# The order of the weight quarters and the modulation blocks in the first product of a two-layer encoder

## The chip, the cores and the metric

The kernel runs on one core of one Trainium2 chip. The metric is the time of one execution on the device in microseconds; the time of a kernel is the median of its runs. The profile is that of one further execution.

## The reference

The kernel computes a two-layer bidirectional encoder on 256 tokens of width 2048, all in float32. What matters here is the beginning of each layer:

```python
cond = jax.nn.silu(c)
mod = cond @ w_ada[l] + b_ada[l]                   # 2048 -> 6 * 2048
sh_a, sc_a, g_a, sh_m, sc_m, g_m = split(mod, 6)
h = _rmsnorm(x) * (1.0 + sc_a) + sh_a
proj = h @ w_in[l]                                 # 2048 -> 3904 columns
```

`proj` is cut into queries, keys and values of a differential attention and into the small latents of a second attention; both attentions, an output projection and a squared-ReLU MLP follow, and then the second layer. The change touches layer 0's part of the lines shown.

## The kernel before

**Tiles.** Everything is held transposed: features on the 128 partitions, the 256 tokens along the free axis. The 2048 features are 16 blocks of 128 ("k"), and the first product takes them two at a time, as pairs 0 to 7 (`p`, with `k = 2 * p`).

**Modulation.** `w_ada` is read as blocks of 128 outputs by 2048 inputs, 1 MB each. `ada_load` issues one such load on SyncE's queue (L294); `ada_sums` has VectorE multiply the block with `cond` and sum along the free axis (L304, two instructions: the product and the read of its sum). After the second block of a pair a small instruction adds the bias (L317 for a shift, L315 for a scale). A pair of feature blocks needs two blocks of the shift ("sh", group 0) and two of the scale ("sc", group 1). `ada_todo` lists them in the order sh, sh, sc, sc, pair by pair. `ada_need(l, g, i)` loads and sums everything in that list up to block `i` of group `g`.

**The operand.** `modulated` makes the two blocks of a pair: `ht` is x times scale times the reciprocal norm (VectorE, L646); the high part of `h` comes from ScalarE (L649) and the low part from VectorE (L650), so that a product can be done as three fast ones (high by high, high by low, low by high). For pairs 0 to 5 (`WHOLE = 6`) ScalarE also makes an unsplit copy `hf` (L654).

**The products of a pair.** `by_k` multiplies the pair's rows of the weights with the operand and adds into open PSUM banks. For pairs 0 to 5 the weights are used unsplit (L233 loads them into four tiles, L244 multiplies). For pairs 6 and 7 `weights` loads a raw tile (L163), ScalarE makes its high part (L148) and VectorE its low part (L151), in two halves, and `mac` issues the three matmuls (L187, L188, L189). Here `io["w_a"]` holds two column groups of 768, `b = 0` and `b = 1`.

**The second columns.** Another 512 columns of the first product, `io["w_d"]`, come as four quarters, each for four feature blocks, always split. Below they are called q0 to q3. `EARLY` says that q0 is done behind pair 4, q1 behind pair 5, q2 behind pair 6; q3 comes behind pair 7. So q0 to q2 use only feature blocks that have long been made.

**Buffers.** Raw tiles and modulation blocks share five buffers of 1 MB (`tag="raw"`); a buffer comes free when VectorE has summed the block or subtracted both halves of the weights. High and low parts have four buffers each (`tag="hi"`, `tag="lo"`), which the unsplit weights of pairs 0 to 5 use as well; they come free when TensorE is through with them.

**What sets the order.** Each engine, and SyncE's queue of loads, works in order. A planner writes that order out before the run: it goes through the program with estimated durations and gives each engine, of the instructions that it takes to be ready, the one that stands first in the program. `follow(ins, after)` forces an order between two instructions of one engine. In the kernel before, at the end of pairs 4, 5 and 6, the program has first all four modulation blocks of the next pair (`ada_need` for sh and sc), then the quarter (`early[p]`), then the next pair's operand. The variable `self.lo` is the last low part that was made, `self.summed` the last sum of a modulation block.

`norm_then_by_k` is called once more, for the MLP of layer 0, with `early` empty.

## Time and profile before

| | |
|---|---|
| median of 3 runs | 2191.54 us (2191.27 to 2192.47) |
| the profiled execution | 2190.2 us |
| its span | 2188.4 us |
| granted TensorE clock, mean | 0.995 |
| TensorE busy (matmuls) | 2158.3 us, 99% |
| VectorE busy | 1610.4 us, 74% |
| ScalarE busy | 1153.3 us, 53% |
| sums of modulation blocks, L304 | 192, of 2284 ns |
| moved by DMA | 586.41 MB, 268 GB/s in the mean |

A row of a timeline reads: start in us from the span's start, duration, engine, line of the kernel, operation, output<-inputs with their shapes, how many in a row; in brackets, how long the engine stood idle before it, and what ended that. PE is TensorE, DVE VectorE, ACT ScalarE, SPq SyncE's queue of loads. A row of a table by stretches reads: the stretch, its length, busy time (and instructions) of PE, of its weight loads, of DVE, ACT and POOL, the granted TensorE clock, the share of DMA, GB/s. The layer's first product lies between 24 us and 152 us of the span.

### The profile page before, as it was taken

Reading aid. Unit: us, or ns where it says so; the run is one execution under the profiler, and the core shown is the slowest. Engines: PE = TensorE matmul, PEld = TensorE weight load, DVE = VectorE, ACT = ScalarE, POOL = GpSimd, SP = SyncE. Lnnn points to the kernel's source line nnn. Section 1 sums busy time; section 2 is a strip of 40 time slices with the busy share of each in tenths; the row PEclk is TensorE's granted clock in tenths of the full one; section 3 lists DMA queues with packets and bytes.
Section 4 is the critical chain, followed back from the end, with each engine's and each line's share of the span. In section 5 each row is a group of like instructions: output and inputs, shape, how many; then the busy total and the mean of one; then the engine's idle time right before and its main releaser. Section 6 shows DMA issues by size and latency. Waiting matters only on the chain.

```text
span 2188.4 us, 30328 instructions
## 1 busy us (share of the span) xinstructions
PE 2158.3 (99%) x11984; PEld 1889.1 (86%) x11984; DVE 1610.4 (74%) x2162; ACT 1153.3 (53%) x1737; POOL 23.8 (1%) x43
## 2 busy tenths in 40 slices
PE   8999999999999999999999999999999999999998
PEld 6899889998888888888898888999888888888886
DVE  8988978888678788788798876798545545545566
ACT  6555664454455355355456565647446535534544
POOL 0000000000000000000001000000000000000000
PEclk9999999999999999999999999999999999999999
DMA  9986888799888889888867666687555555555552
GB/s 399 414 309 249 345 327 293 265 359 353 310 319 325 329 302 341 322 312 319 312 231 271 251 249 231 233 306 247 190 195 185 191 195 188 188 193 192 189 196 95
DMA packets 85538, 586.41 MB, mean 268 GB/s; under 512 B 9489, under 2 KB 9489, under 8 KB 19345
## 3 DMA queue, kind: packets, MB, share of 16 engines
q1 hardware_dynamic: 85106, 583.84, 72.6%
q8 instruction: 94, 1.54, 0.3%
q10 hardware_dynamic: 288, 0.62, 0.1%
q14 instruction: 50, 0.41, 0.1%
HBM read 582.32 MB, written 2.10 MB: 267 GB/s over the span
## 4 chain that ended last, share of the span: by engine, by line
PE 91%; DVE 5%; ACT 2%; issue 0%; DMA 0%; DVEq 0%; ACTq 0%
PE ps L208 24%; PE ps L211 13%; PE py L1061 11%; PE py L1059 11%; PE py L1063 11%; DVE ada L304 3%; PE pk L189 2%; PE pk L187 2%; PE pk L188 2%; PE pv L258 2%; PE pv L259 2%; PE pv L260 2%; PE pa L189 1%; PE pa L187 1%; PE pa L188 1%; DVE lo L151 1%
## 5 line engine op out<-in xcount | busy, mean ns | idle before, releaser
L151 DVE TENSOR_TENSOR lo<-raw,hi 128x1024 fp32r<-128x1024 f32 (+1 forms) x720 | 849.4, 1194 | 473.9 <-ACT hi L148 302.5
L148 ACT ACTIVATE hi<-raw 128x1024 fp32r<-128x1024 f32 (+1 forms) x720 | 737.6, 1035 | 646.4 <-PE py L1063 357.3
L208 PE MATMUL ps<-h,hi 128*128 128x512 f32 x2016 | 471.0, 390 | 0.9 <-ACT hi L148 0.9
L208 PEld LDWEIGHTS ps<-h,hi 128*128 128x128 f32 x2016 | 375.0, 188 | 76.9 <-ACT hi L148 1.3
L304 DVE SCALAR_TENSOR_TENSOR ada<-ada,cond 128x2048 f32<-128x2048 f32 x192 | 437.5, 2284 | 3.1 <-DMA ada<-in_w_ada 3.1
L1059 PE MATMUL py<-hi,hid 128*128 128x512 f32 x1024 | 326.5, 390 | 0.0
L1061 PE MATMUL py<-lo,hid 128*128 128x512 f32 x1024 | 325.9, 389 | 0.0
L1063 PE MATMUL py<-hi,hid 128*128 128x512 f32 x1024 | 325.7, 389 | 0.0
L211 PEld LDWEIGHTS ps<-h,lo 128*128 128x128 f32 x2016 | 250.2, 192 | 4.9
L211 PE MATMUL ps<-h,lo 128*128 128x256 f32 x2016 | 251.7, 283 | 0.0
L1061 PEld LDWEIGHTS py<-lo,hid 128*128 128x128 f32 x1024 | 192.3, 188 | 40.3 <-DVE lo L151 0.4
L1063 PEld LDWEIGHTS py<-hi,hid 128*128 128x128 f32 x1024 | 192.2, 188 | 40.0
L1059 PEld LDWEIGHTS py<-hi,hid 128*128 128x128 f32 x1024 | 191.3, 188 | 38.8
L1098 ACT ACTIVATE sum<-ps 128x256 f32<-128x256 f32 x110 | 42.0, 382 | 122.4 <-PE ps L211 122.4
L187 PE MATMUL pk<-h,hi 128*128 128x256 f32 x304 | 87.4, 293 | 5.2 <-ACT hi L148 3.6
L189 PE MATMUL pk<-h,lo 128*128 128x256 f32 x304 | 87.3, 291 | 1.2 <-DVE lo L151 1.1
L188 PE MATMUL pk<-h,hi 128*128 128x256 f32 x304 | 87.3, 289 | 0.0
L181 DVE TENSOR_TENSOR hid<-relu,hid 128x256 fp32r<-128x256 f32 x128 | 48.3, 421 | 45.8 <-ACT hid L180 45.8
L244 PE MATMUL pk<-hf,w 128*128 128x256 f32 x288 | 64.8, 386 | 6.1 <-ACT hf L654 6.1
L244 PEld LDWEIGHTS pk<-hf,w 128*128 128x128 f32 x288 | 55.5, 194 | 14.7 <-ACT hf L654 6.9
L187 PEld LDWEIGHTS pk<-h,hi 128*128 128x128 f32 x304 | 59.8, 199 | 6.2 <-ACT hi L148 4.4
L189 PEld LDWEIGHTS pk<-h,lo 128*128 128x128 f32 x304 | 59.6, 197 | 2.1 <-DVE lo L151 2.0
(267 smaller groups left out, 2553.3 us busy)
## 6 DMA issues: line engine op xcount, KB each, us to landing
raw<-in_w_m SPq DMA_DIRECT2D x238, 1024.0 KB, 5.0
ada<-in_w_ada SPq DMA_DIRECT2D x192, 1024.0 KB, 5.1
raw<-in_w_ob SPq DMA_DIRECT2D x24, 1024.0 KB, 5.0
raw<-in_w_dv SPq DMA_DIRECT2D x16, 1024.0 KB, 4.8
raw<-in_w_q SPq DMA_DIRECT2D x16, 1024.0 KB, 4.8
raw<-in_w_n SPq DMA_DIRECT2D x16, 768.0 KB, 6.1
w<-in_w_a SPq DMA_DIRECT2D x24, 384.0 KB, 12.6
raw<-in_w_a SPq DMA_DIRECT2D x12, 768.0 KB, 6.2
```

What stands on the lines that cost most here:

```text
L148: ins = nc.scalar.activation(hi, v, AF.Copy)
L151: ins = nc.vector.tensor_tensor(lo, v, hi.bitcast(F32), ALU.subtract)
L187: mm(ps, hi, x[0], start=first, stop=False, skip_group_check=shared)
L188: mm(ps, hi, x[1], start=False, stop=False, skip_group_check=shared)
L189: mm(ps, lo, x[0], start=False, stop=last, skip_group_check=shared)
L208: mm(ps.rearrange("p a b -> p (a b)"), part(w, 0, k), both, start=k == 0, stop=False)
L211: mm(ps[:, 0], part(w, 1, k), x, start=False, stop=k == nk - 1)
L244: self.nc.tensor.matmul(ps, w[i][:, j * P : j * P + P], whole[i], start=first, stop=last, skip_group_check=True)
L304: ins = nc.vector.scalar_tensor_tensor(w, w, 1.0, self.cond, ALU.mult, ALU.mult, accum_out=acc[:, i : i + 1])
L1059: mm(o, xh[:, tok], hi[:, part[j]], start=start, stop=False)
L1061: mm(o, xh[:, tok], lo[:, part[j]], start=False, stop=False)
L1063: mm(o, xl[:, tok], hi[:, part[j]], start=False, stop=stop)
```

## The change

At the end of pairs 4, 5 and 6 the order in the program becomes: the two sh blocks of the next pair, the quarter (load, high parts, low parts, product), then the two sc blocks, whose sums must follow the quarter's low parts on VectorE. The next pair's operand must follow them too (`after=self.lo`, for pairs 5, 6 and 7).

At pair 6, whose weights are split as well, the two sh blocks of pair 7 come earlier still: behind the first column group (`b = 0`) and ahead of the second, with their sums behind the first group's low parts (`after`). `self.hold` then makes the second group's low parts follow the last of these sums. For this, `by_k` is called once per column group instead of once for both; the banks, the order and the number of matmuls that it asks for stay the same. For the MLP's call nothing changes but that.

```diff
 def weights(self, src, width=2048, after=None):
 ...
             ins = nc.vector.tensor_tensor(lo, v, hi.bitcast(F32), ALU.subtract)
+            if self.hold is not None:
+                self.follow(ins, self.hold)
 ...
-    def ada(self, n):
-        self.ada_sums()
+    def ada(self, n, after=None):
+        self.ada_sums(after)
         for _ in range(n):
             self.ada_load()
-            self.ada_sums()
-
-    def ada_need(self, l, g, i):
+            self.ada_sums(after)
+
+    def ada_need(self, l, g, i, after=None):
 ...
-            self.ada(self.ada_todo.index((l, g, i)) + 1)
+            self.ada(self.ada_todo.index((l, g, i)) + 1, after)
 ...
             whole = [] if p < nwhole else None
-            h += self.modulated(r, k, self.mod[l, sh], self.mod[l, sc], whole)
-            self.by_k(banks, [src[l, p, b] for b in range(2)], h, k, NK, 2 * n, whole)
+            h += self.modulated(r, k, self.mod[l, sh], self.mod[l, sc], whole, self.lo if p - 1 in early else None)
+            mid = p in early and whole is None
+            for b in range(2):
+                self.by_k(banks[b * n :], [src[l, p, b]], h, k, NK, 2 * n, whole)
+                if mid and b == 0:
+                    self.ada_need(l, sh, k + 3, self.lo)
+                    self.hold = self.summed
+            self.hold = None
             if fill:
                 fill.pop(0)()
             if p in early:
-                for g in (sh, sc):
-                    self.ada_need(l, g, k + 3)
+                self.ada_need(l, sh, k + 3)
                 early[p](h)
+                self.ada_need(l, sc, k + 3, self.lo)
         return h, banks
```

## The prediction

> **What bounds the kernel now.** I read the page first: how full TensorE is, and what the chain of work that ended last consists of.

> ```profile
> span 2188.4 us, 30328 instructions
> PE 2158.3 (99%) x11984; PEld 1889.1 (86%) x11984; DVE 1610.4 (74%) x2162; ACT 1153.3 (53%) x1737; POOL 23.8 (1%) x43
> ...
> PE 91%; DVE 5%; ACT 2%; issue 0%; DMA 0%; DVEq 0%; ACTq 0%
> ```

> TensorE bounds the kernel as a whole, so an edit saves time only by removing TensorE's own waits, or the slow clock that follows them. The change touches layer 0's first product alone, so the second view is TensorE's waits from 20 to 160 us, as total, times, longest.

> ```profile
> PE pk L244 <- ACT hf L654: 6.1, 1, 6.1
> PE pk L187 <- ACT hi L148: 3.0, 2, 2.4
> PE pk L189 <- DVE lo L151: 1.1, 2, 0.6
> ```

> The 6.1 us is the wait for the very first operand, ahead of everything changed. The other two rows are waits for a split weight tile: 3.0 + 1.1 = 4.1 us. The timeline of TensorE says whose tiles they are (start, duration, idle time before it):

> ```profile
> 83.89 10.52 PE L244 MATMUL pk<-hf,w 128*128 128x256 f32 x48
> 94.99 0.39 PE L187 MATMUL pk<-h,hi 128*128 128x256 f32 x1 [0.58 <-ACT hi L148]
> 96.25 0.39 PE L189 MATMUL pk<-h,lo 128*128 128x256 f32 x1 [0.52 <-DVE lo L151]
> 101.63 10.52 PE L244 MATMUL pk<-hf,w 128*128 128x256 f32 x48
> 111.80 0.47 PE L187 MATMUL pk<-h,hi 128*128 128x256 f32 x1
> ...
> 128.95 0.38 PE L187 MATMUL pk<-h,hi 128*128 128x256 f32 x1 [2.41 <-ACT hi L148]
> 130.25 0.38 PE L189 MATMUL pk<-h,lo 128*128 128x256 f32 x1 [0.56 <-DVE lo L151]
> ...
> 131.34 0.42 PE L187 MATMUL pk<-h,hi 128*128 128x256 f32 x1
> 132.84 0.41 PE L188 MATMUL pk<-h,hi 128*128 128x256 f32 x1
> ...
> 149.84 0.28 PE L188 MATMUL pk<-h,hi 128*128 128x256 f32 x1
> 151.40 0.28 PE L189 MATMUL pk<-h,lo 128*128 128x256 f32 x1
> ```

> The product of pair 4 (83.89) ends at 94.4; then quarter 0 of the second columns, "q0", comes at 94.99 and waits 0.58 and 0.52. The product of pair 5 follows at 101.63, then q1 and pair 6 from 111.80 without a wait. Then q2 waits 2.41 and 0.56, and the last matmul of q3 starts at 151.40. Behind q2's waits the pace breaks: from 131.34 to 132.84 lie 7 steps, 0.214 us each; from 149.84 to 151.40 lie 13, 0.120 each. The table by stretches gives the reason (busy time of the engines, granted clock, DMA):

> ```profile
> 126.50:131.20 4.70, 1.73 (x13) 1.49 (x13) 4.60 (x11) 3.76 (x6) 0.00 (x0) 1.00 1.02 417
> 131.30:134.60 3.30, 3.30 (x18) 3.30 (x17) 3.22 (x7) 1.08 (x2) 0.00 (x0) 0.50 0.89 315
> 410.00:420.00 10.00, 10.00 (x69) 10.00 (x68) 7.41 (x14) 4.69 (x9) 0.00 (x0) 0.77 0.12 24
> ```

> For 3.3 us the granted clock is 0.50: 3.3 / 0.214 = 15.4 matmuls, each 0.094 too long, lose 1.45 us. While TensorE stood (126.50 to 131.20) VectorE was busy for 4.60 of 4.70 us and the DMA share was 1.02: TensorE waited for VectorE's turn. What stands in VectorE's queue is the fourth view, with ScalarE's and the load queue's rows behind it:

> ```profile
> 81.75 0.88 DVE L646 SCALAR_TENSOR_TENSOR ht<-x,mod,rstd 128x256 f32<-128x256 f32 x2
> ...
> 88.23 2.28 DVE L304 SCALAR_TENSOR_TENSOR ada<-ada,cond 128x2048 f32<-128x2048 f32 x1
> ...
> 92.96 0.88 DVE L646 SCALAR_TENSOR_TENSOR ht<-x,mod,rstd 128x256 f32<-128x256 f32 x2
> 94.03 0.48 DVE L650 SCALAR_TENSOR_TENSOR h<-ht,mod,h 128x256 fp32r<-128x256 f32 x1 [0.18 <-ACT h L649]
> 94.97 2.36 DVE L151 TENSOR_TENSOR lo<-raw,hi 128x1024 fp32r<-128x1024 f32 x2 [0.46 <-ACT hi L148]
> ...
> 100.45 2.29 DVE L304 SCALAR_TENSOR_TENSOR ada<-ada,cond 128x2048 f32<-128x2048 f32 x1 [0.51 <-DMA ada<-in_w_ada]
> ...
> 105.34 2.29 DVE L304 SCALAR_TENSOR_TENSOR ada<-ada,cond 128x2048 f32<-128x2048 f32 x1 [0.15 <-DMA ada<-in_w_ada]
> ...
> 109.87 2.36 DVE L151 TENSOR_TENSOR lo<-raw,hi 128x1024 fp32r<-128x1024 f32 x2 [0.46 <-ACT hi L148]
> ...
> 112.55 1.82 DVE L151 TENSOR_TENSOR lo<-raw,hi 128x768 fp32r<-128x768 f32 x2
> 115.82 0.96 DVE L151 TENSOR_TENSOR lo<-raw,hi 128x768 fp32r<-128x768 f32 x1 [1.45 <-ACT hi L148]
> ...
> 126.92 0.88 DVE L646 SCALAR_TENSOR_TENSOR ht<-x,mod,rstd 128x256 f32<-128x256 f32 x2
> ...
> 128.97 2.35 DVE L151 TENSOR_TENSOR lo<-raw,hi 128x1024 fp32r<-128x1024 f32 x2
> ...
> 140.45 1.23 DVE L151 TENSOR_TENSOR lo<-raw,hi 128x1024 fp32r<-128x1024 f32 x1
> ...
> 145.03 1.23 DVE L151 TENSOR_TENSOR lo<-raw,hi 128x1024 fp32r<-128x1024 f32 x1 [2.49 <-ACT hi L148]
> ```

> ```profile
> 83.08 0.89 ACT L654 ACTIVATE hf<-ht,mod 128x256 f32<-128x256 f32 x2
> 84.09 2.39 ACT L481 ACTIVATE bias<-pb 32x512 f32<-32x512 f32 x4
> ...
> 93.90 1.99 ACT L148 ACTIVATE hi<-raw 128x1024 fp32r<-128x1024 f32 x2
> ```

> ```profile
> 81.54 0.33 SPq L163 DMA_DIRECT2D raw<-in_w_d x1
> ...
> 86.67 8.10 SPq L233 DMA_DIRECT2D w<-in_w_a  x4
> 94.86 1.33 SPq L294 DMA_DIRECT2D ada<-in_w_ada  x3
> ```

> VectorE sums all four modulation blocks of the next pair (two shift, "sh", two scale, "sc"; 2.2 us each, 4.4 for two), multiplies that pair's operand ("ht", 92.96 and 126.92), and only then subtracts for the quarter (94.97 and 128.97), though TensorE wants the quarter before that operand. ScalarE, free from 86.5, made q0's high parts only at 93.90, behind ht.

> **The change, part by part.** No arithmetic is added or removed. For pairs 5, 6 and 7 the order becomes sh, sh, quarter, sc, sc, operand, on the load queue and on VectorE. Each issue that is moved costs SP 0.33 us, and all loads of a pair are the same as before.

> *q0.* Until 88.2 VectorE does what it did. The third of the four sums then began (88.23) with no wait, so the third load had landed; that place is now the quarter's. ScalarE is free from 86.5 (84.09 + 2.39) and makes both high parts in 1.99, one ahead of VectorE's turn. The low parts go from 88.3 to 90.6, the two sc sums (4.4, with their small add 0.2) to 95.2, the operand's ht from 95.3; its unsplit form is there 2.2 later (81.75 to 83.08 + 0.89), at 97.5. TensorE takes q0 at 94.4 without a wait: 48 matmuls x 0.120 = 5.8, to 100.2. The operand is 2.7 us early. Saved: 0.58 + 0.52 = **1.1 us**.

> *q1.* There is nothing to save; the question is whether it does harm. The sums at 100.45 and 105.34 both waited for landings, two loads apart: 2.45 us a load. In the new order sh lands at 100.45, q1 at 102.9, the two sc at 105.3 and 107.8. VectorE sums to 102.7, waits for the load and one high part (1.0) until 103.9, subtracts to 106.3, sums to 110.7; ht at 110.9, the whole operand 2 us later at 112.9. TensorE does pair 5 from 100.2 to 110.4 (10.2, as 101.63 to 111.80) and q1 to 116.2. 3.3 us of cover: **0**.

> *Pair 6, with the new wait.* The first half of pair 6's columns is subtracted to 114.7 (1.82), the two sh sums take until 119.2, and only then may the second half's low parts run (the hold), 119.2 to 120.1 and to 121.0. TensorE ends the first half's 36 matmuls at 116.2 + 4.3 = 120.5. Cover: 0.4 us. Behind the held subtraction stand q2's, the sc sums and pair 7's operand; the old kernel subtracted the second half from 115.82 on. Cost between 0 and 1; I take **0**.

> *q2.* Its low parts run from 121.0 to 123.4, the sc sums and their add to 128.0, ht from 128.0, the first operand with both parts at 129.5 (1.5 from ht to the end of the first low part, as 92.96 to 94.51). TensorE ends pair 6 at 124.8, does q2 without a wait until 130.6, and finds the operand: 1.1 us of cover. Saved: 2.41 + 0.56 = **3.0 us**, and with them the slow clock, **1.45 us**.

> [...]

> *What is late next.* VectorE still has the low parts of pair 7's columns, the rotary table's steps and q3's low parts to do; before, it reached q3 at 140.45 and had the first half's low part 1.23 later. Its work up to there is the same. Of its idle time before (1.45, 0.51, 0.46, 0.46 and 0.15 in the rows) the new order keeps 0.9 ahead of the landing at 100.45 and 1.2 ahead of q1, so it gains about 0.9 and has q3's low part at about 140.75. TensorE, from 130.6, ends pair 7's 72 matmuls (8.6) at 139.3 and wants it about 0.5 later, at 139.8 (q2's first matmuls with the high part ran before its low part was there, too). Cost between 0 (the planner puts that subtraction ahead of the rotary steps) and 1.9 (nothing gained); I take the count's own **0.9**.

> *Behind the stage* TensorE is busy nearly throughout, so what is gained stays; but a granted clock of 0.77 stands at 410 to 420, and how much of that drop falls on matmuls can shift when the stage moves by 5 us. 0 is taken; the bounds are -1.45 and +1.45, the price of the drop at 131.

> *The sum*: 1.1 + 3.0 + 1.45 - 0.9 = 4.65 us. The profiled execution took 2190.2 us around its span of 2188.4; it becomes 2185.55. It stands 1.3 below the median of the three runs, 2191.54, so on that scale the forecast is **2186.9 us**.

> **The rivals.** (1) *VectorE becomes the bound.* Splitting a quarter between the sums puts a landing, ScalarE's 1.0 and a slot's release into VectorE's chain three times, and cover is 0.4 at pair 6's second half and 1.1 at pair 7. For it: VectorE 4.60 of 4.70 us busy and the landings that it waited for. Against it: q0 and q1 have over 2 us. If VectorE is 3 us late at pair 7, TensorE waits about 2 there: 2186.9 + 2.0 = 2188.9.

> (2) *The clock drop stays* (the gate needs something else than this gap). For it: the first pair of waits, 0.58 and 0.52, had no drop, so a gap alone isn't enough. Against it: the drop begins right behind the larger pair. 2186.9 + 1.45 = 2188.35.

> (3) *The change doesn't reach the end*: VectorE reaches q3 no earlier than 140.45 and the rest of the stage is paced by its chain. For it: the same work in one engine. Against it: behind q3's first half VectorE had 2.49 us of idle time (145.03), which a late stage can use up first. The 4.65 shrink to about 0.5: 2191.

> (4) *Slower.* In the load queue the two sc blocks now come behind q0, and behind those stand pair 5's whole weights, which wait for TensorE from 86.67 to 94.77. If the planner places the sc blocks behind them, as it already places three blocks of the pair after (94.86), the first lands at 100.45 and the next at 102.9; the sums end at 105.2, pair 5's operand comes at 107.6, and TensorE, free at 100.2, waits 7.4 and loses 1.45 to the clock. With 4.65 saved elsewhere: 2191.5 + 7.4 + 1.45 - 4.65 = 2195.7. It decides once the first sc block lands 3 us after VectorE's turn for it at 90.6. Against it: buffers for them were free by 81.54, where the quarter was issued, 5 us ahead of those weights.

> **How the numbers follow.** The forecast gets 0.56, rival (1) 0.16, (2) 0.06, (3) 0.10, (4) 0.12. The forecast's own range is 2185.9 to 2188.2: the q3 term from 0 to 1.9, and a little at pair 6. The range for 8 in 10 reaches down to 2184.9 (the q3 term at 0, part of the shift at 410) and up to 2192.0, which takes in (1) to (3) and leaves (4) out. About 0.2%, 4.4 us, is what can be told from no change, so faster begins at 2187.1: two thirds of the forecast and a little of the rest, by the shift at 410: 0.44. Slower begins at 2195.9: most of (4), whose price is as likely above as below, and a second stall that it would start: 0.10. The rest, 0.46, is no change that can be told.

> **What would show it.** Right: no wait at q0 and q2 in TensorE's waits, so that the rows for hi and lo shrink from 4.1 us to under 1.5; granted clock 1.00 from 131 to 135; VectorE's low parts of a quarter ahead of the second pair of sums each time; the last matmul of q3 at 146 to 147 instead of 151.40. Wrong: a new wait on h or hf ahead of pair 5 or 7 (rivals 4 and 1), a wait on lo inside pair 6 (the hold), or a q3 that ends at 146 with a span that isn't shorter (the gain lost behind the stage).

## The result and the profile after

| | before | after |
|---|---|---|
| median of 8 runs | 2191.54 us | 2184.72 us |
| lowest to highest | 2190.46 to 2192.47 | 2184.21 to 2185.69 |
| the profiled execution | 2190.2 us | 2184.65 us |
| its span | 2188.4 us | 2182.9 us |

The ratio on record is 0.9974 (the two medians alone give 0.9969) with an interval of 0.9965 to 0.9983, or 3.7 to 7.7 us less than 2191.5. The median, 6.8 us less, lies 2.2 us under the forecast of 2186.9 and 0.2 us under the lower end of the wider predicted range, 2184.9; the profiled execution, 5.55 us less, lies 0.9 under the predicted 2185.55.

The lines of the page that answer to those of before:

```profile
span 2182.9 us, 30328 instructions
...
PE 2156.0 (99%) x11984; PEld 1887.3 (86%) x11984; DVE 1609.2 (74%) x2162; ACT 1151.9 (53%) x1737; POOL 20.0 (1%) x43
```

TensorE's waits from 20 to 160 us:

```profile
PE pk L247 <- ACT hf L657: 6.3, 1, 6.3
PE pk L192 <- DVE lo L152: 1.0, 1, 1.0
```

The four waits for q0 and q2, 4.1 us, are gone. A new one stands there: 1.0 us for a low part. (The change moves line numbers: L149 and L152 were L148 and L151; the other lines shown here move by three, so that L247 was L244, L190 to L192 were L187 to L189 and L307 was L304.) TensorE's timeline says where, and the table by stretches what became of the clock:

```profile
85.00 10.52 PE L247 MATMUL pk<-hf,w 128*128 128x256 f32 x48
...
95.17 0.47 PE L190 MATMUL pk<-h,hi 128*128 128x256 f32 x1
...
101.11 10.53 PE L247 MATMUL pk<-hf,w 128*128 128x256 f32 x48
...
123.75 0.39 PE L192 MATMUL pk<-h,lo 128*128 128x256 f32 x1 [1.04 <-DVE lo L152]
...
147.70 0.28 PE L192 MATMUL pk<-h,lo 128*128 128x256 f32 x1
```

```profile
131.00:135.00 4.00, 4.00 (x34) 3.82 (x33) 3.93 (x10) 3.17 (x6) 0.00 (x0) 1.00 1.02 424
```

Call the **stage** what lies between the starts of the first matmul of pair 4's product and of the last of q3. Before it took 151.40 - 83.89 = 67.5 us, now 147.70 - 85.00 = 62.7: 4.8 us less. q0 follows pair 4 without a wait, the clock is 1.00 where it was 0.50, and the second column group of pair 6 waits 1.04 us. VectorE's timeline shows what is late there:

```profile
89.42 2.36 DVE L152 TENSOR_TENSOR lo<-raw,hi 128x1024 fp32r<-128x1024 f32 x2
...
101.65 2.29 DVE L307 SCALAR_TENSOR_TENSOR ada<-ada,cond 128x2048 f32<-128x2048 f32 x1 [3.27 <-DMA ada<-in_w_ada]
104.12 2.29 DVE L307 SCALAR_TENSOR_TENSOR ada<-ada,cond 128x2048 f32<-128x2048 f32 x1 [0.17 <-DMA ada<-in_w_ada]
...
107.74 2.36 DVE L152 TENSOR_TENSOR lo<-raw,hi 128x1024 fp32r<-128x1024 f32 x2 [1.12 <-ACT hi L149]
...
114.75 0.89 DVE L649 SCALAR_TENSOR_TENSOR ht<-x,mod,rstd 128x256 f32<-128x256 f32 x2
...
118.08 2.29 DVE L307 SCALAR_TENSOR_TENSOR ada<-ada,cond 128x2048 f32<-128x2048 f32 x1
...
122.73 4.10 DVE L152 TENSOR_TENSOR lo<-raw,hi 128x768 fp32r<-128x768 f32 x4
...
131.49 0.88 DVE L649 SCALAR_TENSOR_TENSOR ht<-x,mod,rstd 128x256 f32<-128x256 f32 x2
...
138.80 1.23 DVE L152 TENSOR_TENSOR lo<-raw,hi 128x1024 fp32r<-128x1024 f32 x1
...
141.75 1.22 DVE L152 TENSOR_TENSOR lo<-raw,hi 128x1024 fp32r<-128x1024 f32 x1
```

The order is the one that the change asks for: q0's low parts at 89.42, q1's at 107.74, and at 122.73 the second group's two and q2's two (one row, which bears the shape of its first), before ht at 131.49. But VectorE stood 3.27 us for the first sh block of pair 6. At 122.73 it is 3.5 us behind the 119.2 of the prediction; 1.1 of these are the later start of pair 4 in this profile. The load queue after, and then the same place before, give the reason:

```profile
80.42 2.54 SPq L297 DMA_DIRECT2D ada<-in_w_ada  x2
87.78 8.10 SPq L236 DMA_DIRECT2D w<-in_w_a  x4
95.97 0.86 SPq L297 DMA_DIRECT2D ada<-in_w_ada  x2
96.92 0.38 SPq L166 DMA_DIRECT2D raw<-in_w_d  x1
```

```profile
85.93 0.33 SPq L294 DMA_DIRECT2D ada<-in_w_ada  x1
86.67 8.10 SPq L233 DMA_DIRECT2D w<-in_w_a  x4
```

Before, the planner had put one block of pair 6 (85.93) ahead of pair 5's whole weights, whose issues take 8.1 us, 6.9 of them waiting for TensorE. Now both sh blocks of pair 6 stand behind them, at 95.97.

### The profile page after: what moved, and what is told of

It reads as the page before. It is cut to its first block, busy times and chain, and to the rows that moved or that the text cites. A ratio compares the mean times of both kernels' runs of the same rounds, so it can differ in the third digit from the quotient of the medians.

```text
span 2182.9 us, 30328 instructions
## 1 busy us (share of the span) xinstructions
PE 2156.0 (99%) x11984; PEld 1887.3 (86%) x11984; DVE 1609.2 (74%) x2162; ACT 1151.9 (53%) x1737; POOL 20.0 (1%) x43
## 4 chain that ended last, share of the span: by engine, by line
PE 91%; DVE 5%; ACT 2%; DMA 1%; issue 1%; DVEq 0%; ACTq 0%
PE ps L211 25%; PE ps L214 13%; PE py L1070 11%; PE py L1068 11%; PE py L1072 11%; DVE ada L307 3%; PE pv L261 2%; PE pv L263 2%; PE pv L262 2%; PE pk L192 1%; PE pk L190 1%; PE pk L191 1%; PE pa L192 1%; PE pa L190 1%; PE pa L191 1%; DVE lo L152 1%
## 5 line engine op out<-in xcount | busy, mean ns | idle before, releaser
L152 DVE TENSOR_TENSOR lo<-raw,hi 128x1024 fp32r<-128x1024 f32 (+1 forms) x720 | 849.6, 1196 | 467.2 <-ACT hi L149 294.0
L149 ACT ACTIVATE hi<-raw 128x1024 fp32r<-128x1024 f32 (+1 forms) x720 | 737.1, 1035 | 657.8 <-PE py L1072 357.2
L307 DVE SCALAR_TENSOR_TENSOR ada<-ada,cond 128x2048 f32<-128x2048 f32 x192 | 437.6, 2286 | 5.8 <-DMA ada<-in_w_ada 5.6
L190 PE MATMUL pk<-h,hi 128*128 128x256 f32 x304 | 85.5, 289 | 2.2 <-ACT h L652 1.5
L192 PE MATMUL pk<-h,lo 128*128 128x256 f32 x304 | 85.4, 286 | 1.3 <-DVE lo L152 1.3
L247 PE MATMUL pk<-hf,w 128*128 128x256 f32 x288 | 66.2, 391 | 6.3 <-ACT hf L657 6.3
L247 PEld LDWEIGHTS pk<-hf,w 128*128 128x128 f32 x288 | 56.6, 197 | 15.0 <-ACT hf L657 6.7
L190 PEld LDWEIGHTS pk<-h,hi 128*128 128x128 f32 x304 | 58.3, 195 | 2.9 <-ACT h L652 1.8
L1117 ACT ACTIVATE relu<-sum 128x512 f32<-128x512 f32 x55 | 34.6, 630 | 48.3 <-DVE sum L1109 48.3
```

The lines of the kernel that those rows point to most:

```text
L149: ins = nc.scalar.activation(hi, v, AF.Copy)
L152: ins = nc.vector.tensor_tensor(lo, v, hi.bitcast(F32), ALU.subtract)
L190: mm(ps, hi, x[0], start=first, stop=False, skip_group_check=shared)
L192: mm(ps, lo, x[0], start=False, stop=last, skip_group_check=shared)
L247: self.nc.tensor.matmul(ps, w[i][:, j * P : j * P + P], whole[i], start=first, stop=last, skip_group_check=True)
L307: ins = nc.vector.scalar_tensor_tensor(w, w, 1.0, self.cond, ALU.mult, ALU.mult, accum_out=acc[:, i : i + 1])
```

## The experiments

The stages are worked out as above, from the first and the last matmul in each kernel's own timeline.

| kernel | stage, us | TensorE's waits in it, us | ratio to before, interval |
|---|---|---|---|
| before; profiled again | 67.5; 67.2 | 4.1; 4.0 | |
| the change; profiled again | 62.7; 62.6 | 1.0; 0.9 | 0.9974 (0.9965 to 0.9983) |
| new order at pair 6 alone | 62.5 | 1.1 | 0.9974 (0.9964 to 0.9984) |
| new order at pairs 4 and 5 alone | 68.7 | 4.9 | 1.0006 (0.9997 to 1.0015) |
| without sh between pair 6's groups | 62.8 | 1.4 | 0.9980 (0.9971 to 0.9989) |
| the change, loads issued earlier | 60.9 | 0 | 0.9969 (0.9958 to 0.9981) |
| before, with the gap at q2 filled | 66.0 | 1.6 | 0.9996 (0.9987 to 1.0006) |

Each variant's ratio is to executions of the kernel before that were made beside it, with medians of 2190.19 us and, for the last row, 2190.10. The intervals of the times are wider than most differences between the variants, so the variants are told apart by the stage, each from one profile.

**The new order at pair 6 alone.**

```diff
-                self.ada_need(l, sh, k + 3)
-                early[p](h)
-                self.ada_need(l, sc, k + 3, self.lo)
+                if p == 6:
+                    self.ada_need(l, sh, k + 3)
+                    early[p](h)
+                    self.ada_need(l, sc, k + 3, self.lo)
+                else:
+                    for g in (sh, sc):
+                        self.ada_need(l, g, k + 3)
+                    early[p](h)
```

(`modulated` follows `self.lo` at pair 7 alone.)

> The new order at pair 6 alone (sh sums ahead of the second column group, q2 ahead of the sc sums and of pair 7's operand); pairs 4 and 5 keep the old order. Measure: the stage from the first matmul of pair 4's product to the last of q3, 67.5 us before and 62.7 with the whole change. Theory A (VectorE and the loads are as tight as TensorE, so the parts do not add: what q0 gains is lost again at the wait inside pair 6, because the block ahead of pair 5's weights goes back behind them): q0's waits of 1.1 us stay, there is no wait inside pair 6 and none at q2, and the stage is 62.5, as short as with the whole change; time about 2186 to 2187. Rival B (each quarter pays for itself, the parts add): 67.5 less the 3.2 us that pair 6 and q2 give in the whole change, 64.3, time about 2188.

TensorE's waits from 60 to 160 us, and the stage's ends:

```profile
PE pk L190 <- ACT hi L149: 0.6, 1, 0.6
PE pk L192 <- DVE lo L152: 0.5, 1, 0.5
```

```profile
85.09 0.38 PE L247 MATMUL pk<-hf,w 128*128 128x256 f32 x1
...
147.60 0.28 PE L192 MATMUL pk<-h,lo 128*128 128x256 f32 x1
```

q0 waits as before, nothing waits inside pair 6 or at q2, and the stage is 62.5, as theory A had it, and not rival B's 64.3. The time, 2184.48 us, is lower than the 2186 to 2187 expected. The new order at pair 6 is worth as much as the whole change.

**The new order at pairs 4 and 5 alone.**

```diff
-            mid = p in early and whole is None
+            mid = False
 ...
-                self.ada_need(l, sh, k + 3)
-                early[p](h)
-                self.ada_need(l, sc, k + 3, self.lo)
+                if p < 6:
+                    self.ada_need(l, sh, k + 3)
+                    early[p](h)
+                    self.ada_need(l, sc, k + 3, self.lo)
+                else:
+                    for g in (sh, sc):
+                        self.ada_need(l, g, k + 3)
+                    early[p](h)
```

(`modulated` follows `self.lo` at pairs 5 and 6 alone.)

> The new order at pairs 4 and 5 alone; pair 6 as before the change (all four sums, then pair 7's operand, then q2). Theory A (parts do not add): q0's waits go (-1.6 us with the gaps around them), but VectorE comes later to pair 6 by the 3.3 us that it waited for a load, so TensorE waits about 5 us for q2 instead of 3.0 and the clock drops behind it as before: the stage is 67 to 68.5, time within 1 us of before. Rival B (parts add): stage 65.9, time about 2190.

VectorE's wait, pair 7's operand, and TensorE's wait at q2:

```profile
100.15 2.29 DVE L307 SCALAR_TENSOR_TENSOR ada<-ada,cond 128x2048 f32<-128x2048 f32 x1 [2.92 <-DMA ada<-in_w_ada]
...
127.69 0.88 DVE L649 SCALAR_TENSOR_TENSOR ht<-x,mod,rstd 128x256 f32<-128x256 f32 x2
```

```profile
129.72 0.58 PE L190 MATMUL pk<-h,hi 128*128 128x256 f32 x1 [4.85 <-ACT hi L149]
```

The waits of 1.1 us saved at q0 come back as a wait of 4.85 us at q2 in the place of 2.41 and 0.56, and the stage is 1.2 us longer than before. Of theory A's reason a part is off: measured from the stage's start, VectorE begins q2's low parts only 0.8 us later than before, not 3.3; TensorE is there 1.6 us earlier. The parts do not add: this kernel's stage is a little above theory A's 67 to 68.5 and far from rival B's 65.9. The time, 2190.72 us, cannot be told from before.

**Without the sh sums between pair 6's column groups.** The quarter stays ahead of sc and of the operand everywhere.

```diff
-            mid = p in early and whole is None
+            mid = False
```

> The whole change but for its inner part: at pair 6 both column groups are split first, then the sh sums, then q2, then the sc sums. Theory A: the wait of 1.0 us inside pair 6 goes (1.6 us with the slow steps around it), q2's low parts are 2 us later and TensorE, also earlier, waits up to 1 us for them: stage 61.5 to 62.5, clock 1.00 throughout. Rival C (the sh sums must come between the groups): a wait of 2.5 us at q2 with the clock drop behind it, stage 65.

```profile
132.53 0.62 PE L190 MATMUL pk<-h,hi 128*128 128x256 f32 x3 [0.91 <-ACT h L652]
133.65 0.39 PE L191 MATMUL pk<-h,hi 128*128 128x256 f32 x1 [0.50 <-DVE h L653]
```

The wait inside pair 6 goes, as theory A said, but 1.4 us come back at pair 7's operand and not at q2, and the stage, 62.8, misses the range of 61.5 to 62.5. Rival C's wait of 2.5 us at q2 and its stage of 65 do not come. VectorE is late by the same amount (its ht for pair 7 begins at 131.45, with the whole change at 131.49), and TensorE meets that lateness at the next place. Where the sums stand inside pair 6 decides nothing here. No run leaves out `hold` alone.

**Pair 6's sh loads ahead of pair 5's weights.**

```diff
                 self.ada_need(l, sc, k + 3, self.lo)
+                if p == 4:
+                    for _ in range(2):
+                        self.ada_load()
```

> The whole change, and the loads of pair 6's two sh blocks are issued ahead of pair 5's whole weights instead of behind them. Theory A (the wait inside pair 6 comes from VectorE's 3.3 us without work, which comes from these loads standing behind weights that wait for TensorE): VectorE's wait for the load falls under 1 us, the wait inside pair 6 goes, the stage is 61.1 to 61.5, time 1.3 us under the changed kernel's. Rival D (VectorE's own work, not the load, makes it late): the wait of 1.0 us stays, stage 62.7.

The load queue, VectorE at the second sh sum of pair 6 and at q1's low parts, and the stage's ends:

```profile
79.63 9.13 SPq L297 DMA_DIRECT2D ada<-in_w_ada  x4
88.86 6.27 SPq L236 DMA_DIRECT2D w<-in_w_a  x4
```

```profile
99.44 2.28 DVE L307 SCALAR_TENSOR_TENSOR ada<-ada,cond 128x2048 f32<-128x2048 f32 x1
...
103.24 2.36 DVE L152 TENSOR_TENSOR lo<-raw,hi 128x1024 fp32r<-128x1024 f32 x2 [1.31 <-ACT hi L149]
```

```profile
84.25 10.52 PE L247 MATMUL pk<-hf,w 128*128 128x256 f32 x48
...
145.16 0.28 PE L192 MATMUL pk<-h,lo 128*128 128x256 f32 x1
```

VectorE no longer waits for a load, q1's low parts begin at 103.24 instead of 107.74 (0.75 us of it from an earlier pair 4), and TensorE has no wait at all between 60 and 160 us. The stage is 145.16 - 84.25 = 60.9, 1.8 us under the change's and a little under theory A's 61.1 to 61.5: the two loads behind the weights were the cause of the wait inside pair 6, and rival D falls. The time is 2183.23 us, the lowest median of all; the interval of its ratio overlaps that of the change.

**The gap at q2 filled, in the kernel before.**

```diff
+        self.zero = cp.tile([P, P], F32, name="zero")
+        nc.gpsimd.memset(self.zero, 0.0)
 ...
+                if p == 6:
+                    for _ in range(6):
+                        nc_ = self.nc
+                        nc_.tensor.matmul(banks[0][:, 0], self.zero, self.x[:, 0], start=False, stop=False, skip_group_check=True)
                 early[p](h)
```

> The kernel before the change, with six extra unsplit matmuls that add zeros to an open bank, put on TensorE between pair 6's last matmul and q2's first: 2.6 us of work in the place of the 2.41 us wait. Nothing becomes ready earlier. Theory E (the half clock behind q2 is the price of that gap): the granted clock stays 1.00 from 128 to 135 us, and the stage from pair 4's first matmul to q3's last goes from 67.5 to about 66.3 (less 1.45 for the clock, plus 0.2 that the filling is too long). Rival F (the drop comes from something else, rival 2 of the prediction): the clock still drops for 3.3 us and the stage is 67.5 to 67.8.

TensorE's timeline (an unsplit matmul leaves two records, so six are twelve) and the stretch in which the clock was low:

```profile
84.12 10.52 PE L244 MATMUL pk<-hf,w 128*128 128x256 f32 x48
...
126.58 2.75 PE L706 MATMUL pk<-x,zero 128*128 128x256 f32 x12
129.14 0.39 PE L187 MATMUL pk<-h,hi 128*128 128x256 f32 x1
...
130.44 0.39 PE L189 MATMUL pk<-h,lo 128*128 128x256 f32 x1 [0.56 <-DVE lo L151]
...
150.10 0.28 PE L189 MATMUL pk<-h,lo 128*128 128x256 f32 x1
```

```profile
131.00:135.00 4.00, 4.00 (x36) 4.00 (x35) 3.96 (x7) 1.75 (x3) 0.00 (x0) 1.00 0.92 344
```

The engine works for nothing where it stood idle, nothing comes earlier (q2 begins 45.0 us after the stage's start, before 45.1), and the stage is 66.0 for the expected 66.3: 1.5 us shorter than in the first profile of before and 1.2 shorter than in the second. The half clock was the price of the 2.41 us gap; rival F, the prediction's rival (2), is out. In the whole kernel's time, 2189.38 us, these 1.5 us cannot be told from no change.

**Both kernels profiled once more.**

> The kernel before the change, profiled once more, to see what of the clock belongs to the kernel and what to the execution. Theory G (where the half clock falls behind a gap depends on where a window that runs on its own happens to lie in that execution): the clock from 24 to 38.4 us (0.83 in the first profile) and from 405 to 415 us (0.66) differ from the first profile by several hundredths, worth about 1 us each. Rival H (it belongs to the kernel's own timing): both are within 0.02 of the first profile.

> The changed kernel, profiled once more. Theory G: the clock from 24 to 38.4 us (0.76 in its first profile) and from 405 to 415 us (0.89) differ from the first profile by several hundredths, so that 1.3 us of the difference between the two first profiles at either place was chance. Rival H: both are within 0.02 of the first profile, and the gain of 1.3 us at 405 to 415 is the change's own. In both, the stage is 62.7 with the wait of 1.0 us inside pair 6.

The stage is 67.2 us before and 62.6 with the change, close to the first profiles. But with the change not all was met again: TensorE's waits in the second profile are 0.47 us inside pair 6, where 1.0 was expected, and 0.42 at pair 7's operand:

```profile
PE pk L192 <- DVE lo L152: 0.5, 1, 0.5
PE pk L191 <- DVE h L653: 0.4, 1, 0.4
```

The stretches of the first product's start and of the MLP's norm, in this order: before, before again, the change, the change again. The last column but two is the granted clock. (The stretch from 405 to 415 us that the expectations name gives 0.66, 0.66, 0.89 and 0.75; with the change the low clock begins at 403 us, so a wider one is shown.)

```profile
24.00:38.40 14.40, 12.64 (x52) 10.91 (x53) 14.10 (x24) 10.19 (x18) 0.00 (x0) 0.83 1.02 423
400.00:418.00 18.00, 15.53 (x106) 15.12 (x105) 11.66 (x24) 8.31 (x17) 0.00 (x0) 0.81 0.37 139
```

```profile
24.00:38.40 14.40, 12.52 (x44) 10.52 (x45) 14.13 (x23) 9.87 (x16) 0.00 (x0) 0.72 1.02 426
400.00:418.00 18.00, 15.53 (x110) 14.96 (x109) 11.88 (x24) 8.62 (x17) 0.00 (x0) 0.81 0.41 153
```

```profile
24.00:38.40 14.40, 12.68 (x45) 10.71 (x46) 14.10 (x24) 9.84 (x16) 0.00 (x0) 0.76 1.02 426
400.00:418.00 18.00, 15.56 (x115) 15.23 (x116) 15.01 (x26) 8.22 (x16) 0.00 (x0) 0.91 0.42 146
```

```profile
24.00:38.40 14.40, 11.96 (x45) 10.18 (x46) 14.06 (x23) 9.86 (x16) 0.00 (x0) 0.76 1.02 424
400.00:418.00 18.00, 15.53 (x105) 15.15 (x105) 13.78 (x26) 8.20 (x17) 0.00 (x0) 0.81 0.34 120
```

The same program had 0.83 and 0.72 at the start, and the changed one 0.91 and 0.81 around the norm; the other two pairs are equal (0.76 and 0.81 twice). The clock that the two first traces record says more. Before, the granted clock was 0.50 from 22.01 to 28.84 us, from 131.23 to 134.64 and from 407.71 to 414.54; with the change it was 0.50 from 24.85 to 31.67 and from 403.73 to 407.14; between these stretches, and behind them up to 2175 us, it was 1.00. So the half clock lasted 3.41 or 6.83 us in these two traces, and within each its starts lie whole multiples of 3.41 us apart (32 times and then 81 times before, 111 times with the change). The first stretch of each begins in the same wait of TensorE, the one for the very first operand (19.71 to 25.76 us before, 19.44 to 25.72 with the change), but 2.84 us later with the change, though the two programs are the same up to there. So the starts keep a step of 3.41 us whose place goes with the execution, and that much of theory G these two traces show. From 400 to 420 us the half clock lasted about 6.8 us in five of the nine profiles and about 3.4 in four (twice what the granted clock there lacks to 1.00, summed over the 20 us); the two profiles of the change are one of each. What decides between the two lengths was not shown. Whether the shorter stage favours one of the two stays open: four of the five profiles with a stage under 63 us had the 3.4 us, and none of the other four.

## Why the prediction was right, and where it was not

The stage became 4.8 us shorter where 4.65 were forecast. That the two are so near is luck in part: four terms were off, by -0.5, +1.6, -0.5 and -0.9 us, and nearly cancelled. Each term is measured as the change in how much earlier the same matmul starts in the two first profiles:

| term | forecast | measured |
|---|---|---|
| q0's waits | -1.1 | -1.6 |
| q1 | 0 | 0 |
| the wait inside pair 6 | 0 (0 to 1) | +1.6 |
| q2's waits and the clock | -3.0 and -1.45 | -5.0 together |
| pair 7 | 0 | +0.2 |
| q3 late behind the rotary steps | +0.9 (0 to 1.9) | 0.0 |
| sum | -4.65 | -4.8 |

In the second profiles the wait that the change brings falls elsewhere: pair 6 costs 1.0 and pair 7 0.7.

*The mechanism* held at q0 and q2: quarters ahead of operands fill TensorE's gaps, and the slow clock leaves with the gap (from 131 to 135 us the granted clock is 0.57 in both profiles of before and 1.00 in both of the change). The filled gap shows the clock's part by itself: 1.5 us for the 1.45 that the stretch gave. The half clock stood behind the waits of 2.41 and 0.56 us in the kernel before and at the wait of 4.85 with the new order at pairs 4 and 5 alone (0.50 from 131 to 135). Behind the shorter waits inside the stage the granted clock was 1.00: 0.58 and 0.52 at q0 before, 1.04 in the changed kernel, 0.91 and 0.50 without the inner part.

*q0 and q2* were undersized by half a microsecond each: the sum of the waits leaves out a part of each gap. A wait is counted from the end that the profile gives the matmul before it, while without a wait the next one starts ahead of that end (in the changed kernel q0 starts at 95.17, and pair 4's product ends at 85.00 + 10.52 = 95.52); and the first matmul behind each of the four waits took 0.38 or 0.39 us, the next 0.28.

*The step that failed* is "In the new order sh lands at 100.45, q1 at 102.9", and with it "Cover: 0.4 us" at pair 6. It kept the first sh block of pair 6 ahead of pair 5's weights, where it had been at 85.93. The prediction had looked at exactly this hazard in rival (4), but for the sc blocks of pair 5, which did get ahead (80.42). The block behind them did not: it moved to 95.97, VectorE waited 3.27 us for it, q1's low parts began at 107.74 instead of 103.9 (1.1 us of it is that profile's late start), and the wait inside pair 6 cost 1.6 us, as much as q0 had gained. Issuing both blocks earlier shows that this was the cause. A wait on lo inside pair 6 is one of the signs of being wrong that the prediction names; of its signs of being right, the last matmul of q3 is at 147.70 and not at 146 to 147, by the 1.1 us that this profile came late to pair 4.

*q3*: I let the rotary steps go first and charged 0.9. The planner wove the low parts into them (138.80 and 141.75), and q3 took TensorE the same 5.6 us as before, without a wait.

*The rivals.* (1) VectorE as the bound is partly true: what TensorE still waits for inside pair 6 and at pair 7 is a late VectorE, but late for want of a load; with the loads moved the same work on VectorE keeps up. (2) fell with the filled gap. (3) fell: at 400 us the same matmuls still start 4.5 us earlier, although that profile was 1.1 us late at pair 4. (4) came in a weak form.

*Behind the stage* some 0.7 us more were gained between 165 and 200 us, in both profiles of the change; the wait of 0.5 us for a norm's sum there is gone. Of the rest of the difference between the first two profiles, 1.1 us were lost ahead of pair 4 and 1.3 gained behind the norm at 405; the second profiles (pair 4 at 85.31 and 85.13; right behind the norm the change loses 0.4) put both down, in the main, to the clock of the execution. That the medians differ by 6.8 us and these profiles by 5.55 is within the interval. Of the 2.2 us by which the median missed the forecast, 1.3 are the step from the profiled execution of before to its median, which the prediction added; the changed kernel has no such step (2184.65 and 2184.72).

## What to carry to other kernels

Where a wait is taken away by reordering, follow each queue that the moved instructions pass, loads first: loads that stood behind weights waiting for TensorE cost 1.8 of the 6.6 us by which the stage could shrink. When two engines and the loads are almost equally full (in the stage before: TensorE busy for 63.4 and VectorE for 58.5 of 67.5 us, a DMA share of 0.90), parts of a change do not add: here one of three places gave the whole gain, the other two alone nothing, and only with the loads moved did all three count. Price a gap of TensorE with the slow clock that the trace shows behind it (here 1.5 us behind 2.41), and read small gains from a stage's length, not from the whole time.
